# Where the second layer's modulation is formed in a two-block transformer kernel: on TensorE in the first block, or on VectorE behind the first FFN

## The chip, the core and the metric

The kernel runs on one core of a Trainium2 chip, in one launch. The metric is device time in microseconds (us), from the first to the last instruction and what lies around them. The engines are TensorE (PE; its weight loads are listed apart as PEld), VectorE (DVE), ScalarE (ACT), GpSimd (POOL) and SyncE (SP), which here only issues transfers. POOL issues some too.

## What is computed

Two blocks over 512 tokens of width 1024. The first mixes with four groups (chunked attention, HGRN2, RWKV-7, RG-LRU) and has an MLP. The second has two layers, each modulated by a conditioning vector: layer 0 runs over 512 tokens and 256 context tokens, layer 1 over the 512 tokens alone. What the change concerns is the modulation, cut from the reference:

```python
sc_x = jax.nn.silu(c)          # c: (1, 1024)
sc_c = jax.nn.silu(c_ctx)      # c_ctx: (1024,)
for l in range(DEPTH_2):       # 2 layers; d = 1024
    mx = (sc_x @ ada_w[l] + ada_b[l]).reshape(bsz, 6, 1, d)   # ada_w[l]: 1024 x 6144
    mc = (sc_c @ ada_w[l] + ada_b[l]).reshape(6, d)
    hx = modulate(rmsnorm(x, norm_g[l, 0]), mx[:, 0], mx[:, 1])
    hc = modulate(rmsnorm(ctx, norm_g[l, 0]), mc[0], mc[1])
    ...
```

`modulate(xn, shift, scale)` is `xn * (1 + scale) + shift`; the third and sixth of the six parts are gates on what the mixer and the FFN (`(silu(h @ w1) * (h @ w3)) @ w2`, hidden width 2816) add to x. All is float32. Layer 1 needs no gates and, behind the first two parts, nothing for the context.

## The kernel before

The program is one list of instructions per engine, in an order that a list scheduler fixes when the kernel is built; an engine takes its list in that order. Generators yield between pieces of work, and `weave(main, (other, share), ...)` advances another generator by `share` steps for each step of the main one, which sets the order in which the work is offered to the scheduler.

Large products are made three times: each operand is split into a high and a low part, and `mm3` (lines 202 to 207) multiplies high by high, high by low and low by high. `weight()` (171 to 200) fetches a 128-column piece of a weight matrix on SP's queue into one of three buffers `wr`, ACT casts the high part `wh` (197), DVE subtracts it for the low part `wl` (198); two buffers each. The second weight pair of the FFN has names of its own, `woh` and `wol`, because it is kept longer. `gemm_F` and its parts (`feats`) produce features on the partitions, `gemm_T` tokens.

The modulation is formed by `ada(K, l)` (1018 to 1060). For each of three groups of 2048 of the 6144 columns it runs over the eight blocks of 128 rows: SP fetches 128 x 2048 numbers (1 MB, line 1028, two buffers `aw`), four matmuls (1030) multiply them with the conditioning vector (stationary 128 x 32, plain fp32) and add up in PSUM. After eight steps ACT copies the row (1033), PE transposes it in four pieces (1036) and DVE adds the bias (1038). That is 24 steps per layer. At the end the gates are turned into rows (1045 to 1053) and written to DRAM, and `gmod`, the norm's gain times (1 + scale), is formed (1055 to 1060). Both layers' generators are chained, `mod = chain(ada(K, 0), ada(K, 1))` (1925), and woven into the first block's mixer: beside RWKV, the projections, HGRN and attention, with shares from the table `W` (1866) and what is left over at `run_all(mod)`.

In the second block, layer 0's mixer output leaves through `Post` (1803 to 1859). For each of the tiles of 128 tokens `Post.tile` multiplies by the gate row (`gainrow`, fetched on POOL's queue at 1816; half of the product on POOL at 1827, half on DVE at 1828), adds to x (1831), normalises (1839; the small root is taken on POOL, 1854), and `flush` hands pairs of tiles to the modulation and transposes (1756, 1766, 1768), which fill `hFh` and `hFl`, the FFN's split input (263, 264).

`ffn` (1212 to 1258) goes over 22 columns of 128 hidden features, j = 0 to 21, in groups of six. For each it takes two weights (gate and up), forms silu(gate) * up in `hraw` (1236) and splits it; after a group, `gemm_T` multiplies by the second matrix and adds to the output (1071). The first two columns are run in parts of the tokens, as these become ready: (512, 768), (0, 256), (256, 512), with the last `flush` ahead of the last part. Layer 1's mixer and FFN follow.

Of the kernel before, what the change touches and what calls it, by code (L numbers as in the profile page):

```python
# [105 lines left out]
class Ctx:  # L106
    def __init__(self, tc, I, es):
        self.tc, self.nc, self.I, self.es = tc, tc.nc, I, es
        self.n = 0
        self.odd = False  # L110
        self.pair = "pb"
        self.mem = {}
        nc = self.nc
        self.cp = es.enter_context(tc.tile_pool(name="cp", bufs=1))
        self.wp = es.enter_context(tc.tile_pool(name="wp", bufs=2))
        self.sp = es.enter_context(tc.tile_pool(name="sp", bufs=4))
        self.dp = es.enter_context(tc.tile_pool(name="dp", bufs=1, space=DRAM))
        self.mhalf = self.cp.tile([128, 16], F32, name="mhalf")
        nc.vector.memset(self.mhalf, -0.5)
# [47 lines left out]

    def small(self, shape, tag="sm", bufs=8, dt=F32):
        return self.sp.tile(shape, dt, name=self.nm(tag), tag=tag, bufs=bufs)

    def weight(self, src, step=None, cuts=None, cols=None, own=None, room=None):
# [3 lines left out]
        nc = self.nc  # L175
        nk = src.shape[1]
# [841 lines left out]
def ada(K, l):  # L1018
# [5 lines left out]
    for s in range(3):  # L1024
# [10 lines left out]
        for b in range(4):  # L1035
# [5 lines left out]
                        .unsqueeze(3).to_broadcast([128, 4, 4, 2]), op=ADD)  # L1041

    for gi, (blk, ng) in enumerate(((16, 1), (40, 3))):
        g = K.ap.tile([128, 2, 8], F32, name=K.nm("gate"), tag="gate", bufs=2)
        v.tensor_tensor(out=g, in0=mod[:, blk:blk + 8].rearrange("p b t -> p t b"),
                        in1=K.colsl("ng", 32 * l + 8 * ng, 32 * l + 8 * ng + 8).unsqueeze(1).to_broadcast([128, 2, 8]), op=MUL)
        for t in range(2 if l == 0 else 1):
            q = K.ps("ad")
            nc.tensor.transpose(q[0:8, 0:128], g[:, t], K.ident)
            r = K.ap.tile([8, 128], F32, name=K.nm("grow"), tag="grow", bufs=2)  # L1050
# [161 lines left out]
def ffn(K, P, H, hF, acc, l, nt, size, bufs, own, order, parts, flush, between, done):  # L1212
# [13 lines left out]
    for a, b in hidden_groups(22, size):  # L1226
        h1 = []
        for j in range(a, b):
# [22 lines left out]
            if early == 4:  # L1251
                ahead(last, j - 18)
            elif j == 21:
                last(3)
        if b < 22:
# [608 lines left out]
CAT = 2  # L1864
LAG = (0, 0, 1, 0)
W = (1.211, 0.404, 0.247, 0.348, 0.356, 0.28, 0.383, 0.424, 0.474)
# [11 lines left out]
def block1(K, x1):  # L1878
# [7 lines left out]
    with tc.tile_pool(name="m0", bufs=1, side="right") as m0:  # L1886
# [38 lines left out]
        mod = marked(K, "ada", chain(ada(K, 0), ada(K, 1)))  # L1925
# [121 lines left out]
def silu_c(K):  # L2047
# [5 lines left out]
    for t, key in enumerate(("c", "cc")):  # L2053
        nc.scalar.activation(s, K.colsl(key), AF.Sigmoid)
        v.tensor_tensor(out=K.sc[:, :, t], in0=K.colsl(key), in1=s, op=MUL)
    K.mod = [K.cp.tile([128, 48, 2], F32, name=f"mod{l}") for l in range(2)]
# [111 lines left out]
def block2(K, hF, hfp, finish, x1, out):  # L2168
# [14 lines left out]
    with tc.tile_pool(name="f0", bufs=1) as mp:  # L2183
# [14 lines left out]
        def between():  # L2198
            hp.__exit__(None, None, None)
            hF1.append(hF_tile(Pool(K, hfp.__enter__())))  # L2200
        ffn(K, P, H1, hF, acc, 0, 6, 6, 7, 2, CTX_FIRST, PARTS, po.flush, between, lambda i: po4.tile(i, acc[i]))
# [128 lines left out]
```

## Time and profile before

| | us |
|---|---|
| three runs | 2575.95, 2575.99, 2566.33 |
| median | 2575.95 |
| the execution profiled, its own time | 2575.95 |
| its span, first to last instruction | 2574.0 |
| first block, mixer up to the end of line 1030's work | 0 to about 395 |
| join of layer 0's mixer and its FFN | 1232 to 1292 |
| layer 0's FFN | about 1268 to 1738 |

The mean granted clock of PE is 0.984 of full speed (1.00 is 2.4 GHz, 0.50 is 1.2 GHz). PE is busy for 96% of the span, DVE 47%, ACT 39%, POOL 12%; 271.01 MB move, 4.33 of them on POOL's queue. A row of a group of instructions reads: line, engine, operation, written<-read by the program's names, shapes, count | busy us, mean ns of one | idle time of the engine ahead of them and what ended it. A timeline row begins with start and duration in us. `PE ... x8` counts records; four matmuls of line 1030 leave eight.

### The profile page before, as it was taken

To read this page: it belongs to the slowest core of one execution; us is meant where nothing else is said; L and a number is where in the kernel's file an instruction comes from. 1 tells how busy PE (TensorE), PEld (TensorE's weight loads), DVE (VectorE), ACT (ScalarE), POOL (GpSimd) and SP (SyncE) were. 2 spreads that over 40 slices of the span, in tenths; PEclk is the share of its full clock that TensorE was granted. 3 is DMA by queue.
4 is the path that set the end of the run, shared out by engine and by line. 5 is a ranking of instruction groups with operands and counts; after the bars stand their busy time and mean duration, and the time that the engine had idled before them with its cause. 6 is when DMAs were issued, how large, how long until landed. Compare 5 with 4: busy or idle time off the path is not lost. (4 is left out here: it accounts for less than half of the span.)

```text
span 2574.0 us, 41866 instructions
## 1 busy us (share of the span) xinstructions
PE 2465.3 (96%) x17332; PEld 2064.7 (80%) x17332; DVE 1205.7 (47%) x2151; ACT 998.5 (39%) x1848; POOL 305.4 (12%) x393
## 2 busy tenths in 40 slices
PE   8999989999999998989899999999899999999998
PEld 6567757899897866768889899898877667898896
DVE  4644564433446466673631222333656664423334
ACT  4742234432324355554522211212555554432222
POOL 1101131000001123221200000000332222000001
PEclk9999979999999999999999999999999999999999
DMA  8764574233334312132412212222321114332332
GB/s 268 261 198 153 177 244 168 91 91 96 93 103 142 85 53 63 46 96 83 148 54 65 71 53 71 66 75 74 109 59 39 40 62 139 95 101 84 100 105 91
DMA packets 268623, 271.01 MB, mean 105 GB/s; under 512 B 23936, under 2 KB 233264, under 8 KB 262288
## 3 DMA queue, kind: packets, MB, share of 16 engines
q1 hardware_dynamic: 267200, 264.01, 33.1%
q0 software_dynamic: 1232, 4.33, 0.5%
q8 instruction: 136, 2.23, 0.4%
q14 instruction: 55, 0.45, 0.1%
HBM read 231.90 MB, written 25.45 MB: 100 GB/s over the span
## 5 line engine op out<-in xcount | busy, mean ns | idle before, releaser
L205 PE MATMUL ps<-hFh,wh 128*128 128x512 f32 (+1 forms) x1752 | 629.7, 361 | 5.3 <-ACT qk_l L1275 2.5
L206 PE MATMUL ps<-hFl,wh 128*128 128x512 f32 (+1 forms) x1752 | 625.8, 358 | 3.1 <-DVE hFl L264 3.0
L207 PE MATMUL ps<-hFh,wl 128*128 128x512 f32 (+1 forms) x1752 | 623.7, 356 | 0.5 <-DVE wl L198 0.5
L198 DVE TENSOR_TENSOR wl<-wr,wh 128x1024 fp32r<-128x1024 f32 (+3 forms) x270 | 309.1, 1145 | 640.9 <-ACT wh L197 639.6
L197 ACT CAST wh<-wr 128x1024 fp32r<-128x1024 f32 (+3 forms) x270 | 265.1, 983 | 700.9 <-PE ps L206 357.9
L205 PEld LDWEIGHTS ps<-hFh,wh 128*128 128x128 f32 x1752 | 332.2, 190 | 71.9 <-issue 12.1
L207 PEld LDWEIGHTS ps<-hFh,wl 128*128 128x128 f32 x1752 | 332.5, 190 | 53.8 <-issue 4.3
L206 PEld LDWEIGHTS ps<-hFl,wh 128*128 128x128 f32 x1752 | 332.7, 190 | 51.6 <-DVE hFl L264 4.7
L205 PE MATMUL ps<-wh,h_h 128*128 128x256 f32 x1174 | 332.2, 283 | 0.1
L206 PE MATMUL ps<-wl,h_h 128*128 128x256 f32 x1174 | 332.0, 283 | 0.0
L207 PE MATMUL ps<-wh,h_l 128*128 128x256 f32 x1174 | 331.9, 283 | 0.0
L205 PEld LDWEIGHTS ps<-wh,h_h 128*128 128x128 f32 x1174 | 225.3, 192 | 1.3 <-ACT wh L197 0.5
L206 PEld LDWEIGHTS ps<-wl,h_h 128*128 128x128 f32 x1174 | 223.5, 190 | 0.7 <-DVE wl L198 0.2
L207 PEld LDWEIGHTS ps<-wh,h_l 128*128 128x128 f32 x1174 | 223.4, 190 | 0.2
L1827 POOL TENSOR_TENSOR yg<-y,gainrow 128x512 f32<-128x512 f32 x28 | 40.6, 1448 | 1324.0 <-DVE y L1117 880.2
L1236 DVE TENSOR_TENSOR hraw<-hraw,ps 128x512 f32<-128x512 f32 (+1 forms) x70 | 40.1, 573 | 175.4 <-PE ps L207 175.4
L206 PE MATMUL ps<-wl,hFh 128*128 128x256 f32 (+1 forms) x304 | 87.2, 287 | 0.5 <-DVE wl L198 0.4
L205 PE MATMUL ps<-wh,hFh 128*128 128x256 f32 (+1 forms) x304 | 87.2, 288 | 0.0
L207 PE MATMUL ps<-wh,hFl 128*128 128x256 f32 (+1 forms) x304 | 87.1, 287 | 0.0
L263 ACT CAST h_h<-hraw 128x512 fp32r<-128x512 f32 (+1 forms) x70 | 36.9, 528 | 123.7 <-DVE hraw L1236 123.7
L1628 DVE TENSOR_REDUCE sm<-ps 128x1 f32<-128x768 f32 x64 | 60.8, 954 | 37.0 <-PE ps L207 35.6
L1632 POOL TENSOR_SCALAR ms<-ms,sm 128x768 f32<-128x768 f32 x64 | 60.2, 944 | 149.3 <-DVE sm L1631 144.4
(643 smaller groups left out, 4229.1 us busy)
## 6 DMA issues: line engine op xcount, KB each, us to landing
wr<-in_ffn_w_dram SPq DMA_DIRECT2D x114, 512.0 KB, 3.9
aw<-in_ada_w_dram SPq DMA_DIRECT2D x48, 1024.0 KB, 5.0
wr<-in_mlp_w_dram SPq DMA_DIRECT2D x60, 512.0 KB, 4.0
wr<-in_w_in_dram SPq DMA_DIRECT2D x25, 512.0 KB, 6.4
x<-xr SPq DMA_DIRECT2D x20, 512.0 KB, 2.6
xr<-x SPq DMA_DIRECT2D x18, 512.0 KB, 3.6
wr<-in_ffn_w_dram SPq DMA_DIRECT2D x36, 256.0 KB, 2.6
wr<-in_ab_w_in_dram SPq DMA_DIRECT2D x16, 512.0 KB, 5.2
```

Source lines behind the costliest of these rows:

```text
L197: nc.scalar.copy(dst(hi), view(raw))
L198: nc.vector.tensor_tensor(out=dst(lo), in0=view(raw), in1=dst(hi).bitcast(F32), op=SUB)
L205: mm(out, a.hi, b.hi, start=start, stop=False)
L206: mm(out, a.hi, b.lo, start=False, stop=False)
L207: mm(out, a.lo, b.hi, start=False, stop=stop)
L263: nc.scalar.copy(s.hi, x)
L1236: v.tensor_tensor(out=raw[:, c], in0=raw[:, c], in1=p, op=MUL)
L1628: v.tensor_reduce(out=mx, in_=p[:, 0:768], axis=AX.X, op=MAX, negate=True)
L1632: nc.gpsimd.tensor_scalar(out=s, in0=s, scalar1=r, scalar2=1.0, op0=MUL, op1=MUL)
L1827: nc.gpsimd.tensor_tensor(out=t[:, h[0]], in0=y[:, h[0]], in1=g[:, h[0]], op=MUL)
```

## The change

Only layer 0's modulation stays in `ada`; the shares of the table `W` that belong to it are halved. Layer 1's is formed by a new generator `ada_rows`, which `weight()` advances: `K.behind(ada_rows(...), SHARE)` is set ahead of layer 0's FFN, each call of `weight()` there advances it by 1.6 steps, and `K.rest()` at j = 21 runs what is left. It goes over 12 groups of 512 columns and the eight blocks of 128 rows in each, 96 steps. In a step POOL issues the transfer of a 128 x 512 block (256 KB) for two steps later into one of three buffers `aw`, and DVE multiplies the block with one number per partition and adds it to `aa0` (and, for the first four groups, with the context's to `aa1`). After the fourth step of the next group `sums` adds up over the partitions: per accumulator four fp32 matmuls with the 128 x 128 piece as stationary operand and one column of ones, and DVE adds the bias. The arithmetic for gates and shifts moves to `ada_end`, unchanged, for both layers. Its core:

```diff
+    def tick(self):
+        if self.bg is not None:
+            self.due += self.share
+            while self.due >= 1:
+                next(self.bg, None)
+                self.due -= 1
...
     def weight(self, src, step=None, cuts=None, cols=None, own=None, room=None):
...
+        self.tick()
...
+def ada_rows(K, P, l):
...
+    nc, v = K.nc, K.nc.vector
+    w = K.I["ada_w_2"][l].rearrange("(k p) n -> p k n", p=128)
+    mod = K.mod[l]
+    at = [(g, k) for g in range(12) for k in range(8)]
+    raws = []
+
+    def load():
+        if at:
+            g, k = at.pop(0)
+            raws.append(P.t("aw", [128, 512], 3))
+            nc.gpsimd.dma_start(out=raws[-1], in_=w[:, k, 512 * g:512 * g + 512])
+
+    def sums(g, acc):
+        q = K.ps("pb")
+        n = len(acc)
+        for t, a in enumerate(acc):
+            for b in range(4):
+                nc.tensor.matmul(q[:, n * b + t:n * b + t + 1], a[:, 128 * b:128 * b + 128], K.one, start=True, stop=True)
+        v.tensor_tensor(out=mod[:, 4 * g:4 * g + 4, 0:n], in0=q[:, 0:4 * n].rearrange("p (b t) -> p b t", t=n),
+                        in1=K.colsl("adab", 48 * l + 4 * g, 48 * l + 4 * g + 4).unsqueeze(2).to_broadcast([128, 4, n]), op=ADD)
+    for _ in range(2):
+        load()
+    due = None
+    for g in range(12):
+        acc = [P.t(f"aa{t}", [128, 512], 2) for t in range(2 if g < 4 else 1)]
+        for k in range(8):
+            load()
+            raw = raws.pop(0)
+            for t, a in enumerate(acc):
+                c = K.sc2[:, k, t:t + 1]
+                if k:
+                    v.scalar_tensor_tensor(out=a, in0=raw, scalar=c, in1=a, op0=MUL, op1=ADD)
+                else:
+                    v.tensor_scalar(out=a, in0=raw, scalar1=c, scalar2=None, op0=MUL)
+            if k == 3 and due:
+                sums(*due)
+            yield
+        due = g, acc
+    yield
+    sums(*due)
+    v.memset(mod[:, 16:48, 1], 0.0)
+    yield
+    ada_end(K, l, lambda shape, dt, name, tag, bufs: P.t(tag, shape, 1), lambda: K.ps("pb"))
+    yield
...
             elif j == 21:
                 last(3)
+                K.rest()
...
+SHARE = 1.6
 LAG = (0, 0, 1, 0)
-W = (1.211, 0.404, 0.247, 0.348, 0.356, 0.28, 0.383, 0.424, 0.474)
+W = (0.606, 0.404, 0.124, 0.348, 0.356, 0.14, 0.383, 0.212, 0.237)
...
-        mod = marked(K, "ada", chain(ada(K, 0), ada(K, 1)))
+        mod = marked(K, "ada", ada(K, 0))
...
         def between():
             hp.__exit__(None, None, None)
+            adp.__exit__(None, None, None)
             hF1.append(hF_tile(Pool(K, hfp.__enter__())))
+        adp = tc.tile_pool(name="ada1", bufs=1, side="right")
+        K.behind(ada_rows(K, Pool(K, adp.__enter__()), 1), SHARE)
         ffn(K, P, H1, hF, acc, 0, 6, 6, 7, 2, CTX_FIRST, PARTS, po.flush, between, lambda i: po4.tile(i, acc[i]))
```

In the changed kernel the line numbers are higher: 198 becomes 215, 205 to 207 become 222 to 224, 1236 becomes 1308, 1828 becomes 1901. How the order of the instructions moves is shown at three places.

DVE at the start of the FFN, before: `yg` is the last tile's product with its gate (line 1828), `wol` the low part of the second weight, `nraw` and `hFl` the FFN's input, `y` the norm.

```order
L1828 TENSOR_TENSOR yg_2159_12631<-y3_2051_11751,gainrow_2111_12397 128x512
L198 TENSOR_TENSOR wol_2190_12690<-wr_2188_12687,woh_2189_12689 128x1024
L264 TENSOR_TENSOR hFl_2055_11761<-nraw_2147_12560,hFh_2054_11760 128x2x256
L264 TENSOR_TENSOR hFl_2055_11761<-nraw_2149_12570,hFh_2054_11760 128x2x256
L1768 TENSOR_SCALAR nraw_2151_12580<-ps_2150_12575,gmod01_1909,mod0_292 128x256
L1768 TENSOR_SCALAR nraw_2153_12590<-ps_2152_12585,gmod01_1909,mod0_292 128x256
L1852 TENSOR_SCALAR sm_2155_12598<-ss2_2154_12595 128x1
L1236 TENSOR_TENSOR hraw_2173_12663<-hraw_2173_12663,ps_2192_12719 128x256
L1839 TENSOR_SCALAR y2_2050_11750<-xr_2140_12539,sm_2156_12600 128x1024
```

The same place in the changed kernel, from the last operation on the third block on; `aa0` and `aa1` are the accumulators, `aw` the blocks.

```order
L1096 SCALAR_TENSOR_TENSOR aa1_2140_12487<-aw_2141_12488,sc2_292,aa1_2140_12487 128x512
L1096 SCALAR_TENSOR_TENSOR aa0_2139_12486<-aw_2145_12498,sc2_292,aa0_2139_12486 128x512
L1925 TENSOR_SCALAR sm_2126_12461<-ss2_2125_12458 128x1
L1096 SCALAR_TENSOR_TENSOR aa1_2140_12487<-aw_2145_12498,sc2_292,aa1_2140_12487 128x512
L1912 TENSOR_SCALAR y3_2012_11564<-xr_2119_12442,sm_2127_12463 128x1024
L1096 SCALAR_TENSOR_TENSOR aa0_2139_12486<-aw_2146_12502,sc2_292,aa0_2139_12486 128x512
L1096 SCALAR_TENSOR_TENSOR aa1_2140_12487<-aw_2146_12502,sc2_292,aa1_2140_12487 128x512
L1096 SCALAR_TENSOR_TENSOR aa0_2139_12486<-aw_2153_12515,sc2_292,aa0_2139_12486 128x512
L1096 SCALAR_TENSOR_TENSOR aa1_2140_12487<-aw_2153_12515,sc2_292,aa1_2140_12487 128x512
L215 TENSOR_TENSOR wol_2161_12536<-wr_2159_12533,woh_2160_12535 128x1024
L1308 TENSOR_TENSOR hraw_2134_12479<-hraw_2134_12479,ps_2163_12565 128x256
```

`wol` stood right behind the last `yg` and ahead of the last splits; now it stands behind all of the post-norm and behind the twelve operations of the modulation's first six steps, of which seven are shown.

POOL's queue at that place in the changed kernel: the roots of the norms (`sm`, line 1927, before 1854), the products with the gate (`yg`), and the transfers; a block's transfer waits until DVE has read the third block before it.

```order
L1927 TENSOR_TENSOR sm_2096_12313<-sm_2095_12311,mhalf_66 128x1
L1075 DMA aw_2137_12482<-in_ada_w_2_dram 128x512
L1075 DMA aw_2138_12484<-in_ada_w_2_dram 128x512
L1075 DMA aw_2141_12488<-in_ada_w_2_dram 128x512
L1900 TENSOR_TENSOR yg_2102_12354<-y2_2011_11563,gainrow_2072_12210 128x512
...
L1889 DMA gainrow_2719_17503<-gate010_3958 128x1024
L1075 DMA aw_2145_12498<-in_ada_w_2_dram 128x512
L1927 TENSOR_TENSOR sm_2117_12413<-sm_2116_12411,mhalf_66 128x1
L1075 DMA aw_2146_12502<-in_ada_w_2_dram 128x512
L1927 TENSOR_TENSOR sm_2124_12453<-sm_2123_12451,mhalf_66 128x1
L1075 DMA aw_2153_12515<-in_ada_w_2_dram 128x512
L1927 TENSOR_TENSOR sm_2127_12463<-sm_2126_12461,mhalf_66 128x1
```

Before, only the roots, the products and `gainrow` stood there. The blocks' transfers now stand ahead of the roots.

PE a little later in the changed kernel, where the first group's sums stand between two products of the FFN.

```order
L223 MATMUL ps_13083<-hFl_11574,wh_13053 128x256
L224 MATMUL ps_13083<-hFh_11573,wl_13054 128x256
L1082 MATMUL ps_13113<-one,aa_2139_12486 128x1 x4
L1082 MATMUL ps_13113<-one,aa_2140_12487 128x1 x4
L222 MATMUL ps_13129<-hFh_11573,wh_13125 128x512
```

The second product followed the first before; there are 12 such places, four with two accumulators and eight with one.

## Rows read from the trace of the kernel before

**Rows 1.** Page of the profile, its first two parts: busy us and shares; PE's tenths in 40 slices.

```profile
PE 2465.3 (96%) x17332; PEld 2064.7 (80%) x17332; DVE 1205.7 (47%) x2151; ACT 998.5 (39%) x1848; POOL 305.4 (12%) x393
...
PE   8999989999999998989899999999899999999998
...
PEclk9999979999999999999999999999999999999999
```

**Rows 2.** Busy time by stretches: PE, PEld, DVE, ACT, POOL (records), PEclk, DMA share, GB/s.

```profile
0.00:128.00 128.00, 114.33 (x583) 74.30 (x583) 73.11 (x147) 74.56 (x101) 15.29 (x33) 1.00 0.80 264
128.00:320.00 192.00, 185.35 (x2904) 140.47 (x2902) 92.50 (x154) 60.55 (x92) 16.64 (x11) 1.00 0.54 178
320.00:400.00 80.00, 72.14 (x724) 43.19 (x724) 44.94 (x127) 27.70 (x63) 21.63 (x27) 0.81 0.65 222
1252.00:1262.00 10.00, 8.39 (x65) 7.72 (x64) 9.35 (x16) 9.09 (x20) 4.77 (x4) 1.00 0.73 216
1262.00:1272.00 10.00, 7.61 (x63) 7.17 (x61) 9.64 (x18) 7.90 (x21) 3.37 (x4) 1.00 0.72 243
...
1290.00:1738.00 448.00, 448.00 (x3011) 414.68 (x3011) 123.40 (x182) 99.41 (x158) 0.00 (x0) 1.00 0.22 65
```

**Rows 3.** Groups by line (busy us, mean ns), and stretches of line 1030 alone.

```profile
L1030 PE MATMUL ps<-aw,sc 128*32 128x512 f32 x384 | 64.0, 647 | 1.4 <-DVE mod L1038 1.4
...
0.00:128.00 128.00, 20.01 (x144) 3.07 (x144) 1.00 0.80 264
128.00:320.00 192.00, 22.29 (x144) 3.23 (x144) 1.00 0.54 178
320.00:400.00 80.00, 21.72 (x96) 2.62 (x96) 0.81 0.65 222
```

**Rows 4.** Timeline of PE (start us, us, operation), one step at either clock.

```profile
151.71 1.06 PE L1030 MATMUL ps<-aw,sc 128*32 128x512 f32 x8
...
375.19 1.93 PE L1030 MATMUL ps<-aw,sc 128*32 128x512 f32 x8
```

**Rows 5.** Busy time by stretches, around the first drop of the clock.

```profile
320.00:324.00 4.00, 1.67 (x34) 1.47 (x34) 3.76 (x11) 0.51 (x3) 0.00 (x0) 0.93 0.74 207
324.00:336.00 12.00, 11.47 (x113) 8.27 (x115) 8.00 (x25) 5.42 (x14) 6.34 (x7) 0.50 0.66 240
```

**Rows 6.** Timeline of PE's weight loads (PEld): four fp32 transposes.

```profile
84.97 0.59 PEld L1036 LDWEIGHTS ps<-c_ident,arow 128*128 128x128 f32 x4
```

**Rows 7.** Page, part 6: DMA issues, KB each, median us to landing.

```profile
aw<-in_ada_w_dram SPq DMA_DIRECT2D x48, 1024.0 KB, 5.0
wr<-in_mlp_w_dram SPq DMA_DIRECT2D x60, 512.0 KB, 4.0
wr<-in_w_in_dram SPq DMA_DIRECT2D x25, 512.0 KB, 6.4
...
wr<-in_ffn_w_dram SPq DMA_DIRECT2D x36, 256.0 KB, 2.6
```

**Rows 8.** Timeline of DVE, then PE, at the start of the FFN.

```profile
1264.24 1.21 DVE L198 TENSOR_TENSOR wol<-wr,woh 128x1024 fp32r<-128x1024 f32 x1
...
1267.61 0.40 DVE L1236 TENSOR_TENSOR hraw<-hraw,ps 128x256 f32<-128x256 f32 x1
...
1273.44 0.75 DVE L1839 TENSOR_SCALAR y<-xr,sm 128x1024 f32<-128x1024 f32 x1 [0.66 <-POOL sm L1854]
...
1268.07 0.38 PE L205 MATMUL ps<-hFh,woh 128*128 128x256 f32 x1 [1.70 <-DVE hraw L1236]
```

**Rows 9.** Groups by line, DVE: busy us, mean ns of one.

```profile
L1831 DVE SCALAR_TENSOR_TENSOR xr<-yg,sm,xr 128x512 f32<-128x512 f32 x56 | 39.7, 749 | 14.7 <-POOL sm L1854 13.1 <-DMA xr<-x 1.4
...
L1839 DVE TENSOR_SCALAR y<-xr,sm 128x1024 f32<-128x1024 f32 x24 | 19.2, 800 | 14.0 <-POOL sm L1854 13.7
```

**Rows 10.** Transfers from POOL's queue at line 1816; DMA issues between 1230 and 1300 us.

```profile
DMA to landing us min/median/max: 4.7/6.6/8.1
...
gainrow<-gate POOLq DMA_DIRECT2D x2, 512.0 KB, 4.7
```

**Rows 11.** Busy time of the whole join, columns as in rows 2.

```profile
1232.00:1292.00 60.00, 51.67 (x415) 49.16 (x415) 41.07 (x72) 36.84 (x90) 17.11 (x19) 1.00 0.46 150
```

More of the change, by code (lines that the diff above doesn't have):

```diff
@@ L112, in __init__ @@
         self.mem = {}
+        self.bg, self.share, self.due = None, 0.0, 0.0
         nc = self.nc
@@ L166, in colsl, with behind, rest @@
         return self.cols[:, at + a:at + (n if b is None else b)]
+    def behind(self, gen, share):
+        self.bg, self.share, self.due = gen, share, 0.0
+    def rest(self):
+        run_all(self.bg)
+        self.bg = None
+    def tick(self):
[4 more added lines that the diff above has]
+                self.due -= 1
     def small(self, shape, tag="sm", bufs=8, dt=F32):
@@ L1041, in ada, with ada_end @@
                         .unsqueeze(3).to_broadcast([128, 4, 4, 2]), op=ADD)
+    ada_end(K, l, K.ap.tile, lambda: K.ps("ad"))
+def ada_rows(K, P, l):
[41 more added lines that the diff above has]
+    yield
+def ada_end(K, l, tile, ps):
+    nc, v = K.nc, K.nc.vector
+    mod = K.mod[l]
     for gi, (blk, ng) in enumerate(((16, 1), (40, 3))):
-        g = K.ap.tile([128, 2, 8], F32, name=K.nm("gate"), tag="gate", bufs=2)
+        g = tile([128, 2, 8], F32, name=K.nm("gate"), tag="gate", bufs=2)
         v.tensor_tensor(out=g, in0=mod[:, blk:blk + 8].rearrange("p b t -> p t b"),
@@ L1047, in ada @@
         for t in range(2 if l == 0 else 1):
-            q = K.ps("ad")
+            q = ps()
             nc.tensor.transpose(q[0:8, 0:128], g[:, t], K.ident)
-            r = K.ap.tile([8, 128], F32, name=K.nm("grow"), tag="grow", bufs=2)
+            r = tile([8, 128], F32, name=K.nm("grow"), tag="grow", bufs=2)
             nc.scalar.copy(r, q[0:8, 0:128])
@@ L2055, in silu_c @@
         v.tensor_tensor(out=K.sc[:, :, t], in0=K.colsl(key), in1=s, op=MUL)
+    K.sc2 = K.cp.tile([128, 8, 2], F32, name="sc2")
+    v.tensor_copy(K.sc2, K.sc[:, :, 0:2])
+    K.one = K.cp.tile([128, 1], F32, name="one")
+    v.memset(K.one, 1.0)
     K.mod = [K.cp.tile([128, 48, 2], F32, name=f"mod{l}") for l in range(2)]
```

## The prediction

> **What bounds the kernel now.** I began with the page's busy shares: TensorE (PE) is busy for 2465.3 of 2574.0 us, 96%, VectorE (DVE) and ScalarE less than half of it, and the 40 slices show PE at eight or nine tenths everywhere [rows 1]. So the first question for every instruction is what it adds to PE, and the second, in the places where PE waits, who is late there. The change touches three places, and I read each by itself, in the view of busy time by stretches [rows 2]. The mixer of the first block (0 to 400 us): PE works 114.3 of 128, 185.4 of 192 and 72.1 of 80 us; in the last stretch its granted clock is 0.81. The first FFN of the second block (1290 to 1738 us): PE works 448.00 of 448.00 us, DVE 123.4, ScalarE 99.4, GpSimd (POOL) nothing, DMA 0.22 of its share. Whatever PE gets there in addition is paid in full, and DVE has room on average. The join of the two (1252 to 1292 us), where layer 0's mixer output is normalised, modulated and split for the FFN: PE works only 8.39 and 7.61 of 10 us, and DVE 9.35 and 9.64 of 10. There DVE is the bound, on 20 us, which the average of the page hides.
>
> The execution profiled took 2575.95 us for a span of 2574.0, and it is also the median of the three (2566.33 to 2575.99), so sums against it are sums against the median. Half a per cent, 12.9 us, is about what a measurement of this kernel can tell from no change.
>
> **1. What leaves the first block: minus 27 us.** The modulation's matmuls (line 1030) are 384 records, 64.0 us [rows 3], for 48 steps of 1 MB; the change takes out the 24 of layer 1. By stretches they are 20.01 us (0 to 128), 22.29 (128 to 320) and 21.72 (320 to 400). The last is dear because of the clock: one step takes 1.06 us at 151.71 and 1.93 at 375.19 [rows 4]. Half of everything is 32.0 us. How much of it comes back depends on what they fill. Up to 320 us PE stands for about 20 of 320 us, and I take 0.85 of (20.01 + 22.29) / 2 = 21.1, so 18.0. From 320 to 400 us PE waits for chains through DVE and POOL: at 320 to 324 it works 1.67 of 4 us and the clock is then 0.50 for 12 us [rows 5]. A step taken out there often leaves a wait, so I take half of 10.9, 5.4. With them go 12 transposes at 0.59 / 4 = 0.15 us [rows 6], 1.8 us, and waits before them of about 1. 24 MB fewer also stand in front of the first block's weights on SP's queue, where these land after 6.4 us against 4.0 for the MLP's [rows 7]; 1. Sum 27. Ends: 12, if only a third of the 32 comes back because the chains set the pace, and 42, if all of it does together with transposes, waits, queue and a little clock (32 + 1.8 + 1 + 4 + 3).
>
> **2. What PE gets in the FFN: plus 13 us.** The new sums are 16 sets of four fp32 matmuls with a 128x128 stationary operand and one column. Line 1030's 48 x 4 matmuls left 384 records, so an fp32 matmul is two passes; 64 matmuls make 128 passes. No such pass is in the trace. From above: the weight loads of four fp32 transposes took 0.59 us, 0.148 each [rows 6], times 128 is 18.9 us. From below: from 128 to 320 us 2904 records took 185.35 us; without line 1030's 144 in 22.29 us that is 163.1 / 2760 = 0.059 us for a small matmul [rows 2, 3], times 128 is 7.6. I take the middle, 13, and keep both.
> Beside the row of 0.148 us stands a rule of the Trainium skill ("TensorE: Matmul & The Clock Gate", section "LDWEIGHTS (loading the stationary operand)"): a load takes its columns divided by 1.2, in ns, 107 ns for 128, however many rows it has. The row is a third longer. By the rule the sums would be an estimated 13.7 us, by the row 18.9.
>
> **3. The start of the FFN: plus 16 us.** The order shows that the scheduler puts DVE's work for the first six steps, 12 operations, among and behind the last ones of the post-norm and ahead of two that PE waits for: the low part `wol` of the second weight, and the `hraw` product. In the kernel before `wol` runs at 1264.24, `hraw` at 1267.61, and PE begins with the first FFN columns at 1268.07 [rows 8]. Count DVE's time: its last operation of the post-norm ends at 1274.2. Off that go `wol` (1.2) and three short ones that now come later (1.2), on it come ten operations like line 1831's, 0.75 us, and two at half of line 1839's 0.80 [rows 9], 8.3 us; 1.0 us of idle time goes into them. So `wol` begins at 1279 and ends at 1280.3.
> Count by the loads too: there are three buffers, and the sixth block is issued on POOL's queue only when DVE has finished with the third, which by the same durations is at 1273.4. What lands from POOL's queue takes 4.7 us at best and 8.1 at worst for 512 KB (part of it written to all partitions), while SP's 256 KB loads take 2.6 [rows 7, 10]; I take 4.7 and get 1278.2, two operations to 1279.6, `wol` to 1280.8. Both counts agree. PE stands at the third matmul of its group from 1268.4 to 1280.8, 12.4 us. Behind `wol` more accumulation stands ahead of the last splits of layer 0's activations, and POOL's norms (`pow`) are queued behind the loads; the first parts then end some 4 us later still. Sum 16. Ends: 7, if the transfers are quick and PE finds work, and 22, if each of the blocks takes 6 us or more.
>
> **4. The clock after that pause: plus 5 us.** A pause of some 2.3 us at 320 to 324 was followed by 12 us at 0.50, which costs 6 [rows 5]. From 1232 to 1292 us 8.3 us of idle time in small pieces left the clock at 1.00 [rows 11]. A pause of 12 us in one piece is nearer to the former. Ends 0 and 8.
>
> **5. The rest of the FFN: plus 3 us.** 128 operations are about 16 x 0.4 + 112 x 0.75 = 90 us on DVE, beside 123 in 448 us; hidden on average. But they come in runs of up to eight steps in 12 to 17 us, in a place where a column block's matmuls leave some 12 us, and PE may meet a late `wl`. 3, ends 0 and 10. 24 MB in 448 us are 56 GB/s beside 65: hidden. The gates' and shifts' arithmetic is only moved, some twenty small instructions, under 1 us.
>
> **Sum:** -27 + 13 + 16 + 5 + 3 = +10, to 2586; since DVE may find a little idle time that I counted as full, I say **2585 us**. The likeliest case's own range is 2573 to 2597.
>
> **Rivals.**
> A. Slower, by the loads. If a block needs 7 to 8 us from issue to landing, the three buffers let only three steps pass in one such time, the six steps of the start last some 26 us instead of 20, every later run of eight steps as well, and PE waits for DVE several times. For it: the median of the eight landings is 6.6 us [rows 10]. Against it: the two at 1230 to 1300 us, beside a DVE that was almost full, took 4.7. It decides from about 6 us upwards. Price: 27 less, 13, 22 and 8 more, and 8 for later runs: +24, **2600 us**.
> A rule of the Trainium skill works in this direction ("SBUF — State Buffer", the box "The 'DVE blocks DMA' trap (SWDGE)"): for a transfer issued from POOL's queue the descriptors are written by GpSimd, which is locked out while DVE runs certain copies at its fast rate. By that rule the landings grow just where DVE is full. The trace's 4.7 us at such a place speaks against it, so far.
> B. Faster, because DVE's order harms little. If blocks land in 2.6 us like SP's and PE fills the pause from the transposes that are due there, the start costs 7, the clock nothing, the sums 8, later runs nothing, and the first block gives 36: -21, **2555 us**. For it: PE is the bound nearly everywhere, which makes removed work worth its time. Against it: DVE's own count above comes to the same end without any transfer.
> C. Slower, because the steps taken out were fillers. Then the first block gives 12 and the rest stands: -12 + 37 = +25, **2601 us**. For it: PE follows chains there, and the 320 to 400 stretch shows the waits. Against it: 96% busy up to 320 us.
>
> **How the numbers follow.** Forecast 0.52, A 0.17, B 0.20, C 0.11. Of the forecast's range, 2573 to 2588.8 is within half a per cent (above 2563.1 and below 2588.8) and about seven tenths of its chance, 0.37; the rest, 0.15, is slower. B gives faster, 0.19 of its 0.20; 0.01 goes to the middle. A and C are slower but for 0.02 each. So faster 0.19, same 0.42, slower 0.39. The range of 8 in 10 takes the forecast's case whole and most of the three others: 2553 to 2607.
>
> **What would show it.** Step 1: line 1030's records halve to 192 and the hand-over from the mixer to what follows comes about 27 us sooner (the first matmul of the FFN then starts near 1241). Step 2: 64 matmuls of one column and 6 to 19 us between the last matmul before and the first one behind them. Step 3: an idle time of PE of 10 to 13 us before the third matmul of the first FFN group, put down to DVE's `wol`; the time from the join's start to the end of the first parts is 16 us longer. Step 4: clock 0.5 to 0.6 behind it. Step 5: from there to the end of the FFN 10 to 25 us more than before, with PE at 97% or more. I am wrong if the pause is under 5 us, if the mixer's gain is under 15 or over 38 us, or if the landings of the new blocks are over 6 us.

## The result, and the profile after

| | us |
|---|---|
| before, median of 10 runs | 2572.57 (2566.33 to 2581.22) |
| changed, median of 10 runs | 2587.07 (2583.57 to 2590.47) |
| ratio | 1.0055, 95% interval 1.0044 to 1.0067 |
| the changed kernel's profiled execution | 2590.2, span 2588.4 |

So the change makes the kernel some 14 us slower, half a per cent. The forecast was 2585 with a range of 2553 to 2607, and its sum was +10. That the sum came out close is partly luck: two terms were too large, in opposite directions, and a cost of 4.5 us was not in it at all. Both profiled executions are some 3 us slower than the medians of their kernels, so they can be compared with each other. The place of each term is seen when they are laid side by side at the same instructions (line numbers of the kernel before):

| place (us from the start of the span) | before | changed | difference |
|---|---|---|---|
| last output of the first block's attention (line 998) | 394.5 | 375.1 | -19.4 |
| first gate row of layer 0's post-norm fetched (line 1816) | 1181.3 | 1161.9 | -19.3 |
| FFN's sixth `hraw` product, the first parts are done (line 1236) | 1298.0 | 1291.2 | -6.8 |
| layer 1's first attention output (line 1641) | 1919.5 | 1928.9 | +9.4 |
| last addition to x (line 1831) | 2569.7 | 2579.6 | +9.9 |
| last instruction | 2574.0 | 2588.4 | +14.4 |

The first block gives 19.4 us. The join and the first parts of the FFN take 12.5 back, the way from there to layer 1's attention 16.2, what follows 0.5, and the last microseconds of the program 4.5.

**The first block.** Busy time in one stretch, from the start to the first matmul behind the attention, which stands at 394.4 us in the kernel before and at 374.9 in the changed one; columns as in [rows 2]. First before, then after:

```profile
0.00:394.40 394.40, 366.22 (x4162) 252.36 (x4162) 208.64 (x426) 161.40 (x251) 52.22 (x69) 0.96 0.64 214
```

```profile
0.00:374.90 374.90, 336.69 (x3956) 246.08 (x3956) 212.93 (x424) 161.11 (x250) 54.05 (x69) 0.95 0.49 161
```

PE works 29.5 us less, but it stands idle for 38.2 us instead of 28.2: ten of the 29.5 us came back as idle time. The modulation's own matmuls in the changed kernel answer to [rows 3]:

```profile
0.00:128.00 128.00, 11.29 (x72) 1.69 (x72) 0.99 0.63 206
128.00:320.00 192.00, 15.02 (x74) 2.34 (x74) 0.96 0.42 135
320.00:400.00 80.00, 10.37 (x46) 1.37 (x46) 0.89 0.51 165
```

Their sum is 36.7 us for half the steps, where half of the 64.0 before would be 32.0. The steps that stay are dearer up to 320 us, where the granted clock is 0.99 and 0.96 and was 1.00. At HGRN's first output (line 872, 322.4 us in the kernel before) the changed kernel is 14.6 us ahead; the last stretch adds 4.8. In the ten runs below that keep this first block (all but the one with the old shares) the profiled executions are 17.3 to 22.9 us ahead at its end, so 19.4 is good to some 3 us.

**The start of the FFN.** The changed kernel's busy time by stretches, then PE's waits from 1225 to 1780 us (who waited for whom: us, times, longest), then the timelines of PE and of DVE:

```profile
1242.00:1252.00 10.00, 4.74 (x34) 4.03 (x32) 9.18 (x17) 6.90 (x17) 5.25 (x6) 0.88 0.59 209
1252.00:1262.00 10.00, 2.85 (x12) 2.48 (x13) 9.43 (x16) 2.30 (x6) 3.59 (x6) 0.50 0.72 245
1262.00:1272.00 10.00, 10.00 (x68) 10.00 (x68) 6.54 (x13) 2.55 (x6) 1.70 (x3) 0.76 0.43 126
```

```profile
PE ps L1829 <- DVE y L1912: 9.4, 2, 6.1
PE ps L224 <- DVE wol L215: 2.2, 1, 2.2
...
PE ps L223 <- DVE wl L215: 1.3, 2, 0.9
```

```profile
1256.97 1.51 PE L1829 MATMUL ps<-c_ident,y 128*128 128x128 f32 x6 [6.09 <-DVE y L1912]
1260.66 0.58 PE L224 MATMUL ps<-hFh,wol 128*128 128x256 f32 x1 [2.17 <-DVE wol L215]
```

```profile
1254.87 0.74 DVE L1096 SCALAR_TENSOR_TENSOR aa<-aw,sc,aa 128x512 f32<-128x512 f32 x1
1256.07 0.76 DVE L1912 TENSOR_SCALAR y<-xr,sm 128x1024 f32<-128x1024 f32 x1 [0.46 <-POOL sm L1927]
1256.74 2.73 DVE L1096 SCALAR_TENSOR_TENSOR aa<-aw,sc,aa 128x512 f32<-128x512 f32 x4
1259.39 1.22 DVE L215 TENSOR_TENSOR wol<-wr,woh 128x1024 fp32r<-128x1024 f32 x1
1260.53 0.41 DVE L1308 TENSOR_TENSOR hraw<-hraw,ps 128x256 f32<-128x256 f32 x1
```

Where DVE's additions (`aa`) stand among the last of the post-norm, PE works 4.74 and 2.85 of 10 us, and its clock falls to 0.50. The corresponding stretches of the kernel before lie 19.4 us later, and PE works 7.61 and 10.00 of 10 us in them:

```profile
1261.40:1271.40 10.00, 7.61 (x63) 7.17 (x61) 9.64 (x18) 7.52 (x19) 3.37 (x4) 1.00 0.70 231
1271.40:1281.40 10.00, 10.00 (x86) 10.00 (x85) 3.19 (x8) 2.65 (x8) 0.54 (x1) 1.00 0.38 134
```

There `wol` [rows 8] came right behind the last `yg`; now it begins 16 us after it (`yg` begins at 1243.35). The additions make two things late: first `y`, the normalised tile that PE transposes (9.4 us in two pieces), then `wol` (2.2).

From the fetch of the gate row to the sixth `hraw` PE runs 892 records in both kernels. Before, then after:

```profile
1181.26:1298.00 116.74, 108.36 (x892) 105.61 (x893) 54.70 (x86) 54.52 (x123) 20.30 (x23) 1.00 0.42 135
```

```profile
1161.95:1291.16 129.21, 112.17 (x892) 109.14 (x893) 74.43 (x118) 54.55 (x123) 32.57 (x42) 0.93 0.50 161
```

PE is idle for 17.0 us instead of 8.4, 8.7 more by the unrounded figures, and busy for 3.8 us more with as many records, at a mean granted clock of 0.93 instead of 1.00. Together that is the loss of 12.5 us there.

**The rest of the FFN.** PE's timeline around a set of sums with two accumulators, and around one with one:

```profile
1315.91 1.84 PE L1082 MATMUL ps<-one,aa 128*128 128x1 f32 x16
1317.61 0.47 PE L222 MATMUL ps<-hFh,wh 128*128 128x512 f32 x1
...
1585.73 0.95 PE L1082 MATMUL ps<-one,aa 128*128 128x1 f32 x8
1586.53 0.47 PE L222 MATMUL ps<-hFh,wh 128*128 128x512 f32 x1
```

A set of eight matmuls leaves 16 records and holds the next product back by 1.70 us (0.106 us per record) and a little before it. I count 1.8 us for each such set and 0.9 for those of half the size, as the lag of `hraw` behind the kernel before grows at single sets; for four and eight sets that is an estimated 14.4 us. Of the 16.2 us that leaves 1.8, of which late `wl` are 1.3.

**The end.** One line stands for what closes the program; among its instructions is POOL's DRAIN, which begins at POOL's last operation. Instructions of that line, with their number, min/median/max in ns, first and last start; before, then after:

```profile
L2326 POOLq DRAIN  x3: 40/102/1492, 2568.4 to 2573.8; - x3
```

```profile
L2407 POOLq DRAIN  x3: 40/93/9334, 2578.3 to 2588.2; - x3
```

In the changed kernel the DMA engines are idle from 2583, but this DRAIN runs from 2578.3 for 9.3 us. Between the issue of the last output and the last instruction there are 8.0 us instead of 3.5.

### The profile page after: what moved, and what is told of

Read it like the earlier page. It is cut to its first block, busy times and chain, and to the rows that moved or that the text cites. A ratio compares the mean times of both kernels' runs of the same rounds, so it can differ in the third digit from the quotient of the medians.

```text
span 2588.4 us, 42092 instructions
## 1 busy us (share of the span) xinstructions
PE 2456.2 (95%) x17256; PEld 2077.3 (80%) x17256; DVE 1290.2 (50%) x2291; ACT 996.8 (39%) x1845; POOL 361.0 (14%) x489
## 4 chain that ended last, share of the span: by engine, by line
PE 72%; DVE 10%; issue 7%; ACT 5%; DMA 3%; POOL 3%; SPq 0%; POOLq 0%; DVEq 0%; ACTq 0%
PE ps L222 20%; PE ps L223 20%; PE ps L224 20%; PE ps L731 3%; PE ps L716 2%; DMA aw<-in_ada_w_dram 2%; DVE wl L215 1%; POOL sm L1927 1%; DVE xr L1904 1%; PE ps L1047 1%; PE ps L1404 1%; ACT wh L214 1%; PE ps L1405 1%; PE ps L834 0%; DVE yg L1901 0%
## 5 line engine op out<-in xcount | busy, mean ns | idle before, releaser
L1075 POOL DMA_DIRECT2D aw<-in_ada_w_dram x96 | 52.5, 547 | 378.1 <-DVE aa L1098 189.4
L1096 DVE SCALAR_TENSOR_TENSOR aa<-aw,sc,aa 128x512 f32<-128x512 f32 x112 | 81.1, 748 | 33.3 <-DMA aw<-in_ada_w_dram 32.6
```

What stands on the lines that cost most here:

```text
L1075: nc.gpsimd.dma_start(out=raws[-1], in_=w[:, k, 512 * g:512 * g + 512])
L1096: v.scalar_tensor_tensor(out=a, in0=raw, scalar=c, in1=a, op0=MUL, op1=ADD)
```

## The experiments

Each time is a median of several runs, its ratio is to the kernel before on the same chip. The changed kernel stands at 1.0055. Where I give a difference in us to it as a span, one end is the difference of the times and the other that of the ratios.

| run | us | ratio, 95% interval |
|---|---|---|
| no modulation of layer 1 | 2554.65 | 0.9929, 0.9914 to 0.9943 |
| begins behind the fourth weight | 2581.82 | 1.0037, 1.0023 to 1.0051 |
| no transfers | 2581.10 | 1.0035, 1.0022 to 1.0048 |
| no sums | 2593.00 | 1.0077, 1.0060 to 1.0095 |
| begins behind the third column | 2576.57 | 1.0020, 1.0009 to 1.0031 |
| a quarter of the sums | 2578.24 | 1.0024, 1.0011 to 1.0036 |
| old shares in the first block | 2587.70 | 1.0061, 1.0045 to 1.0076 |
| third column, sums in rows | 2574.20 | 1.0007, 0.9995 to 1.0019 |
| third column, SP's queue | 2568.88 | 0.9978, 0.9967 to 0.9989 |
| third column, SP's queue, sums in halves | 2562.62 | 0.9949, 0.9933 to 0.9966 |
| changed kernel, SP's queue | 2578.18 | 1.0015, 1.0004 to 1.0026 |

**What the first block gives: no modulation of layer 1 at all.**

```diff
-        K.behind(ada_rows(K, Pool(K, adp.__enter__()), 1), SHARE)
+        adp.__enter__()
+        K.mod[1] = K.mod[0]
+        for i in range(2):
+            K.gate[1, i, 0], K.gmod[1, i] = K.gate[0, i, 0], K.gmod[0, i]
```

> Layer 1's modulation is left out altogether: the first block as in the changed kernel, no blocks, sums or VectorE work in the FFN, and layer 1 takes layer 0's shift, scale and gates. My theory: what leaves the first block gives some 20 us (TensorE's work there 29.5 us less, its waits 10 us more), and all that is added costs 34, of which 12.6 at the start of the FFN and 14.4 for the sums. So 2553 us, 2549 to 2557. Rival 1: all of the 32 us comes back and the trace's loss is this run's own, 2541. Rival 2: the steps were fillers, gain 12 or less, 2561 or more.

Measured 2554.65 us, 0.0071 less than before, 18 us. The gain of the first block is real and stays to the end: the profiled execution is 19.4 us ahead at the end of the first block, 22.4 at the FFN and 22.9 at the last addition. Between the first block and the FFN the edit changes nothing, so the 2 to 3 us gained there are scatter between executions. All that the change adds costs 1.0055 - 0.9929, 32 us.

**What makes the start late: no transfers.** One block serves all steps.

```diff
+    fix = P.t("aw", [128, 512], 1)
+    nc.gpsimd.dma_start(out=fix, in_=w[:, 0, 0:512])
...
-            raws.append(P.t("aw", [128, 512], 3))
-            nc.gpsimd.dma_start(out=raws[-1], in_=w[:, k, 512 * g:512 * g + 512])
+            raws.append(fix)
```

> One block is loaded and used in all 96 steps: no transfers on POOL's queue in the FFN, VectorE's operations and their order unchanged at the start (the modulation of layer 1 is then that of a wrong weight). Theory (VectorE's own work is the bound of the start): within 4 us of the changed kernel, 2583 to 2588. Rival (each step waits for its block, three buffers and one round trip): the start loses most of its 12.6 us, 2573 to 2578.

Measured 2581.10, 5 to 6 us less than the changed kernel and 2 us below what the theory allowed. The intervals of the two ratios just overlap, so the gain is less sure than its cause at the end. The waits at the start did not move. PE's waits of this run, 1225 to 1780 us, and its closing DRAIN:

```profile
PE ps L1831 <- DVE y L1914: 9.3, 2, 6.1
PE ps L224 <- DVE wol L215: 2.2, 1, 2.2
```

```profile
L2409 POOLq DRAIN  x3: 40/93/1574, 2579.8 to 2585.1; - x3
```

9.3 and 2.2 us as in the changed kernel, without a transfer for each step: VectorE's own operations and their order set the start. From the gate row to the first `hraw` this run takes 99.1 us, the changed kernel 98.6 and the kernel before 86.4. Behind that the order did change: the first set of sums and half of the second now stand ahead of the fifth `hraw` (24 records, 3.41 us), and at the sixth the run is 18.0 us behind its place at the gate row. So it holds the start equal only up to the first `hraw`. What was gained is at the end, where the DRAIN is short and the last instruction comes 3.8 us after the last output, not 8.0.

**When it begins.** First by leaving out the first four weights:

```diff
-        self.bg, self.share, self.due = gen, share, 0.0
+        self.bg, self.share, self.due = gen, share, -4 * share
...
-SHARE = 1.6
+SHARE = 1.72
```

> The first four weights of the FFN don't advance the modulation, the others by 1.72 steps instead of 1.6; by the order of instructions VectorE's low part of the second weight and the first product then stand where they stood before the change. Theory (VectorE's additions ahead of what TensorE waits for cost the 12.6 us at the start, clock included): 8 to 11 us come back, 2576 to 2579. Rival (POOL's queue, its transfers ahead of the norms' roots, or the traffic): under 4 us comes back, 2583 or more.

Measured 2581.82: 5 us came back, between the two, and the intervals of this run and the changed kernel overlap. `wol` was in its old place, but the scheduler puts an operation wherever its engine is free by its reckoning, and eleven additions now stood ahead of the last tiles' modulation: PE waited 5.6 us for `nraw` and 3.0 for `hraw`. Between the fetch of the gate row and the ninth `hraw` the run lost 8.1 us, with one set of sums (1.8) among them. So a later place in the program is not a later place in the order. The second try ties the first operation to a product of the third column:

```diff
+            if j == 2 and K.wait is not None:
+                K.wait(raw)
...
+        def start(raw):
+            sc2 = AP.t("sc2b", [128, 8, 2], 1)
+            v.scalar_tensor_tensor(out=sc2, in0=raw[:, 752:768].rearrange("p (k t) -> p k t", t=2), scalar=0.0, in1=K.sc2, op0=MUL, op1=ADD)
+            K.sc2, K.wait = sc2, None
+            K.behind(ada_rows(K, AP, 1), SHARE)
...
```

> The modulation of layer 1 begins only when the third column's product exists: its factors are copied by an operation that reads that product (times zero), so the scheduler can't move a step ahead of it; 1.83 steps per weight. By the order nothing of it stands among the last operations of the post-norm or the splits. Theory (what stands ahead of PE's inputs at the join costs the 12 us; elsewhere TensorE has cover): 20 less for the first block, 14.4 for the sums, 3 for late low parts, 2571 us, 2567 to 2576. Rival (VectorE's runs of additions do the same harm wherever they begin): 2579 or more.

Measured 2576.57, 9 to 10.5 us less than the changed kernel. Its profiled execution is 22.1 us ahead of the kernel before at the gate row, 22.5 at the first `hraw` and still 22.5 at the sixth: the join costs nothing. PE's waits there:

```profile
PE ps L1831 <- ACT nraw L1841: 2.0, 3, 0.9
PE ps L222 <- DVE hraw L1308: 1.7, 1, 1.7
```

The theory's 2571 was missed by 5.6 us, of which I put 4.5 down to the DRAIN, still 9334 ns long, that I had not yet seen.

**What the sums cost.** First all of them taken out:

```diff
-                nc.tensor.matmul(q[:, n * b + t:n * b + t + 1], a[:, 128 * b:128 * b + 128], K.one, start=True, stop=True)
...
+        v.tensor_copy(mod[:, 4 * g:4 * g + 4, 0:n], K.colsl("adab", 48 * l + 4 * g, 48 * l + 4 * g + 4).unsqueeze(2).to_broadcast([128, 4, n]))
```

> The 64 matmuls of the sums are left out, layer 1's modulation is the bias alone. Theory (16 sets at 0.9 us, fully paid since TensorE has no idle time there): 14 us less, 2571 to 2575. Rival (the drift within the FFN is mostly late low parts of weights): 6 us less at most, 2581 or more.

Measured 2593.00, slower than with them; both theories missed. The timeline of DVE in this run shows why:

```profile
1399.53 0.49 DVE L1093 TENSOR_SCALAR aa<-aw,sc 128x512 f32<-128x512 f32 x1 [0.59 <-DMA aw<-in_ada_w_dram]
1400.90 0.75 DVE L1091 SCALAR_TENSOR_TENSOR aa<-aw,sc,aa 128x512 f32<-128x512 f32 x1 [0.88 <-DMA aw<-in_ada_w_dram]
1402.74 0.75 DVE L1091 SCALAR_TENSOR_TENSOR aa<-aw,sc,aa 128x512 f32<-128x512 f32 x1 [1.09 <-DMA aw<-in_ada_w_dram]
...
1408.01 0.75 DVE L1091 SCALAR_TENSOR_TENSOR aa<-aw,sc,aa 128x512 f32<-128x512 f32 x1 [1.59 <-DMA aw<-in_ada_w_dram]
1409.04 1.57 DVE L1091 SCALAR_TENSOR_TENSOR aa<-aw,sc,aa 128x512 f32<-128x512 f32 x2 [0.27 <-DMA aw<-in_ada_w_dram]
1410.52 1.82 DVE L215 TENSOR_TENSOR wl<-wr,wh 128x1024 fp32r<-128x1024 f32 x2
```

```profile
PE ps L223 <- DVE wl L215: 13.1, 3, 7.9
```

The additions stand in one long run, most of them wait for their own transfers, and the weights' low part behind them is late: 13.1 us of PE's time. In the kernel's code an accumulator can't be used again before its sums have read it; I take it that without sums nothing else holds the additions back, but only the order is seen, not its reason. It is rival A's chain of blocks and buffers at another place, though without its long landings: their median in this run is 3.3 us. The edit changed the order, so this run does not price the sums. The next keeps each set in its place with a quarter of its matmuls:

```diff
-            for b in range(4):
-                nc.tensor.matmul(q[:, n * b + t:n * b + t + 1], a[:, 128 * b:128 * b + 128], K.one, start=True, stop=True)
+            nc.tensor.matmul(q[:, t:t + 1], a[:, 0:128], K.one, start=True, stop=True)
...
```

> The changed kernel with one of the four matmuls per accumulator, so 16 instead of 64, its sums used for all four parts (wrong numbers for three quarters); each set still stands where it stood, so VectorE is held in step with TensorE as before. Theory (0.225 us each, paid in full): 48 x 0.225 = 10.8 us less than the changed kernel, 2576, 2573 to 2580. Rival (the sums stand in waits that are there anyway, as the run without any sums, which was slower, could be read): under 4 us less, 2583 or more.

Measured 2578.24: 8 to 9 us less, of the 10.8 that 48 matmuls stand for. Late `wl` rose from 1.3 to 4.5 us at the same time. So the sums are paid nearly in full.

**Whether steps in the first block were fillers: the old shares.** Layer 0's steps are as dense as all steps were before, and done halfway.

```diff
-W = (0.606, 0.404, 0.124, 0.348, 0.356, 0.14, 0.383, 0.212, 0.237)
+W = (1.211, 0.404, 0.247, 0.348, 0.356, 0.28, 0.383, 0.424, 0.474)
```

> The changed kernel with the shares of the table as before the change: layer 0's 24 steps come twice as dense and are done about halfway, none is left for the last stretch of the mixer. Theory (where the chains set the pace a step is a filler that costs little, and a step among full work costs its whole time): the same or up to 8 us slower, 2587 to 2595. Rival (steps at the low clock are the dear ones, it pays to be rid of them): 3 to 7 us faster, 2580 to 2584.

Measured 2587.70, the changed kernel's time within 1 us. The rival falls. Busy time from 320 to 380 us, this run and then the changed kernel:

```profile
320.00:380.00 60.00, 48.74 (x507) 36.16 (x508) 38.41 (x104) 25.23 (x52) 21.53 (x23) 0.72 0.23 76
```

```profile
320.00:380.00 60.00, 52.67 (x554) 33.65 (x551) 37.20 (x105) 25.83 (x57) 19.44 (x24) 0.86 0.49 160
```

Without any step in that stretch PE works less and at a lower clock, and the program is no faster. The steps were mostly fillers there, but not wholly. This run reaches HGRN's first output (line 889 here) at 312.3 us, 4.5 later than the changed kernel, and the last output of attention at 375.2, level with it (375.1). From 308 us on the changed kernel has 16.1 us of line 1047's matmuls (the modulation's, 1030 before) and this run has none, and only 4.4 us come of it. Earlier, 6.8 us more of these matmuls cost it the 4.5.

**A version that is faster.** Three edits on the run that begins behind the third column. The first makes the sums in rows, two accumulators as moving operands against a block of ones:

```diff
+        for i, a in enumerate(acc):
+            nc.tensor.matmul(p[32 * i:32 * i + 32], K.one, a, start=True, stop=True)
+        row = P.t("aw", [128, 512], 3)
+        nc.scalar.copy(row[0:64], p[0:64])
+        q = K.ps("pb")
+        for b in range(4):
+            nc.tensor.transpose(q[:, 64 * b:64 * b + 64], row[0:64, 128 * b:128 * b + 128], K.ident[0:64, 0:64])
...
```

> As the run that begins after the third column, and the sums made in rows: two accumulators at a time are the moving operand against a 128 x 32 stationary block of ones, ScalarE copies the rows and four transposes turn them, as in the first block's modulation; 8 sets of 2 matmuls and 4 transposes. From line 1030's step (1.06 us for four such matmuls) and 0.15 us per transpose I expect 1.1 to 1.5 us per set, 9 to 12 us in all instead of 14.4. Theory: 2 to 5 us faster than the run with the same start, 2566 to 2569 if that comes to 2571. Rival (the way over ScalarE and one buffer of the loads holds VectorE up): no faster than that.

Measured 2574.20 at 1.0007, against 1.0020: 2 to 3 us, with intervals that overlap, so this is not settled. The second only moves the transfers:

```diff
-            nc.gpsimd.dma_start(out=raws[-1], in_=w[:, k, 512 * g:512 * g + 512])
+            nc.sync.dma_start(out=raws[-1], in_=w[:, k, 512 * g:512 * g + 512])
```

> As the run that begins after the third column, but the 96 blocks are fetched on SP's queue instead of POOL's. In all the runs with 96 transfers on POOL's queue the last instructions come 8.0 us after the last output transfer is issued, in those without them 3.6, and POOL's closing DRAIN lasts 9.3 us instead of 1.5. Theory (each transfer on POOL's queue adds some 0.08 us to that DRAIN, 4.5 us of it not hidden): 4.5 us less than that run, 2572, and the DRAIN at 1.5. Rival (the tail belongs to the 24 MB or to the pool's buffers, not to the queue): the tail stays at 8 us, 2576. A loss is possible too: on SP's queue a block that waits for its buffer holds up the weights behind it; then PE waits for `wl` in the FFN, and the time is 2577 or more with a tail of 3.6 all the same.

Measured 2568.88 at 0.9978, 8 to 11 us less than with POOL's queue. The closing DRAIN:

```profile
L2416 POOLq DRAIN  x3: 40/102/1494, 2560.4 to 2565.7; - x3
```

1494 ns, and 3.5 us from the last output to the end; no weight was late behind a block (`wl` 0.6 us). The 4.5 us at the end are shown; where the other 3 to 6 us come from is not, since the profiled executions differ by as much ahead of the FFN, where the edit changes nothing. The third takes the sums in halves, so that four column groups work at once:

```diff
+        for i in range(4):
+            nc.tensor.matmul(p[32 * i:32 * i + 32, 0:256], K.one, acc[i // 2][:, 256 * (i % 2):256 * (i % 2) + 256], start=True, stop=True)
...
+        for b in range(2):
+            nc.tensor.transpose(q[:, 128 * b:128 * b + 128], row[:, 128 * b:128 * b + 128], K.ident)
...
```

> The same, and the sums in rows with four column groups at once: two accumulators in halves of 256 columns, each group of 32 columns of the array taking one half; two transposes instead of four. In the run with rows two groups took 1.05 us for 32 x 512 columns where line 1030's four took 1.06, so half the width at four groups should take 0.53, with two transposes of 0.15 and the gaps about 1.0 us per set, 8 us for 8 sets against 14.4. Theory: 6 us less than the run beside it, 2566. Rival (the sums' price is the break in the stream of matmuls, not their length): no more than 2 us less.

Measured 2562.62, 6 to 7.5 us less than the run beside it (the one above, with the changed kernel's sums), and 0.9949 of the kernel before: with its whole interval below 1, this version beats both, by half a per cent over the kernel before. One set of the run with whole rows, then one of this:

```profile
1338.12 1.05 PE L1080 MATMUL ps<-aa,one 128*32 128x512 f32 x4
...
1340.01 0.46 PE L1085 MATMUL ps<-c_ident,aw 64*128 64x64 f32 x4
```

```profile
1336.02 0.64 PE L1080 MATMUL ps<-aa,one 128*32 128x256 f32 x8
...
1337.54 0.38 PE L1085 MATMUL ps<-c_ident,aw 128*128 128x128 f32 x2
```

1.05 + 0.46 us become 0.64 + 0.38, eight times: an estimated 8.2 us, against the 14.4 for the sums of the changed kernel. The difference of 6.2 is what the time shows.

The last run makes the edit of the queue alone on the changed kernel:

> The changed kernel with one edit: its 96 blocks are fetched on SP's queue. Theory: POOL's closing DRAIN is back at 1.5 us and the time 4.5 us lower, 2582 to 2584, while the wait at the start of the FFN stays within 2 us of what it was, since VectorE's own operations set it. Rival (POOL's queue, with its norms' roots behind the transfers, is part of the wait at the start): 6 us or more lower, 2580 or less.

Measured 2578.18, 9 to 10 us less, more than the theory said and in the rival's range, although the wait at the start moved by only 1.3 us. Its waits at the start are 9.3 us for `y`, where the changed kernel had 9.4, and 0.9 instead of 2.2 for `wol`; in the profiled executions the join and the first parts cost 10.2 us instead of 12.5, the rest of the FFN up to layer 1's attention 12.8 instead of 16.2, the end 4.5 less. So POOL's queue seems to have a small part in the start after all, some 2 us of one profiled execution, and it is in `wol` and not in `y`; why the FFN's end is shorter I can't say.

## Why the prediction was right

**The whole.** 2585 was forecast, 2587 measured, inside the forecast case's own range of 2573 to 2597. The two are nearer than the effects: the forecast stood on 2575.95 for the kernel before and added 9, but the median of ten runs is 2572.57 and the change adds 14.5. By terms it was less good: the gain of step 1 and the cost of steps 3 and 4 were each some 8 us too large, and cancelled, which is luck.

**Step 1, -27: measured -19.4.** The halving was right (29.5 us of PE's work went); the share of 0.85 for the time up to 320 us was not. At HGRN's first output the gain was 14.6, where I had 18.0 up to 320 us for the steps alone; the last stretch gave 4.8 against my 5.4. The share was read from PE's busy time, and that does not say whether the work in it is a filler: 10 us of idle time appeared. The steps that stayed also cost 36.7 us instead of 32.0, which I had not counted. What came back lies midway between my 27 and rival C's 12.

**Step 2, +13: measured 14.4.** Two passes per matmul was right (128 records), and 0.106 us for one lies between the ends of 0.059 and 0.148. The rule that the Trainium skill gives in "TensorE: Matmul & The Clock Gate", section "LDWEIGHTS (loading the stationary operand)", 107 ns for 128 columns, gives an estimated 13.7 us. The trace agrees with it: 0.106 us per record. The row of the transposes, 0.148, was the worse guide.

**Steps 3 and 4, +16 and +5: measured 12.5 together, 8.7 of idle time and 3.8 of low clock.** The place and the cause were right, and the run without transfers shows that DVE's own time decides. The count of DVE's time was right too: `wol` begins at 1259.39, with the first block's 19.4 us added 1278.8, against my 1279, and the product that waits for it comes some 11.6 us later than before, against my 12.4. The reader was not quite right: of 11.6 us of waits 9.4 are for `y`, the norm of the last tiles, which has the additions ahead of it on DVE, and only 2.2 for `wol`. With the transfers on SP's queue the wait for `y` is the same, so POOL's queue is not its cause. The clock fell to 0.50 and was at 0.76 in the next 10 us, as step 4 said, and cost 3.8 of its 5. The mis-sized part is step 3's "some 4 us later still". From the first to the sixth `hraw` the kernel before takes 30.4 us and the changed one 30.6: PE lost time to the low clock there, but it had done ten records more ahead of the first `hraw`, and stood idle for 0.5 us instead of 1.3. So what came late behind the pause added nothing.

**Step 5, +3: measured 1.8.** Late `wl` cost 1.3 us. The run without sums points at what kept it small: by the code each group's additions wait for the sums of the group before the last, which spreads them.

**Not in the sum: 4.5 us at the end**, from the queue of the transfers. My step 5 counted their traffic and nothing else.

**The rivals.** A falls: the blocks landed in 2.8 to 5.8 us, median 3.3 (3.2 to 5.0 for the nine issued up to 1262 us), against 4.7 to 8.1 in [rows 10], and so below the 6 us from which it decides:

```profile
L1075 POOL DMA_DIRECT2D aw<-in_ada_w_dram x96: 536/536/946, 1233.3 to 1679.8; - x96
...
DMA to landing us min/median/max: 2.8/3.3/5.8
```

The rule of the Trainium skill beside it ("SBUF — State Buffer", the box "The 'DVE blocks DMA' trap (SWDGE)") does not decide here either: at the start DVE was busy for over nine tenths, and the landings stayed short. No run separates the copies that the rule speaks of from DVE's other operations, so the rule itself is not tested. B falls by the run without transfers, which loses as much up to the first `hraw`, and by the sums. C's mechanism is seen in the run with the old shares, where 16.1 us of steps were worth 4.4, and in PE's idle time, at 10 us of the 29.5 instead of 20 of 32.

## What to carry to other kernels

Work that is moved off a saturated engine is worth its time only where it did not fill a wait, so ask of each place what the engine does when the work is gone, not how busy it was. On an engine that has room on average, look at the 20 us in which it has none: here the scheduler put operations there whose operands were early, a later place in the program did not keep them out, and a true dependence did. When an experiment removes work, compare the order of the rest before reading the time.

## What the runs showed of the hardware

The DRAIN at the end of POOL's queue grows with the transfers issued there: 1.49 us in the kernel before, 1.57 with one more, 9.33 with 96 more, 1.49 with all 96 on SP's queue. That is 1574 - 1492 = 82 ns for the one and (9334 - 1492) / 96 = 82 ns for each of the 96, so over these three numbers of transfers it is even, although the 96 had landed long before. Here 4.5 us of it showed, because the last work of POOL ends shortly before the end.

Two column groups of 32 with 512 columns took 1.05 us, four took 1.06 in [rows 4], and four with 256 columns 0.64. So two groups took as long as four: with two busy, the other half of the array's width brought nothing.
